# Filler products, halved first loads, a reordered projection tail and an explicit function-table load in the first part of a two-layer decoder kernel

## The chip, the core and the metric

The kernel runs on one core of one Trainium2 chip. The metric is the device time of one execution in microseconds (us), taken as the median of several runs. Engines are named as the profile names them: PE (TensorE, matrix products and transposes), PEld (its weight loads), ACT (ScalarE), DVE (VectorE), POOL (GpSimd) and SP (SyncE, which issues the DMAs).

## What is computed

Two layers over 256 tokens of width 1024, in float32. Layer 0 is attention (three groups of four dilated-window heads and one group of differential heads, all with normed queries and keys) and a dense SwiGLU. Layer 1 is a gated linear recurrence (HGRN2) and a mixture of 8 experts of which each token takes 2. Cut to its frame, the reference is:

```python
for layer in range(DEPTH):
    if layer % 2 == 0:
        h = h + dilated_diff_mixer(rms_norm(h, attn_norm[j]), attn_w_in[j], ..., attn_w_out[j], layer)
        h = h + swiglu(rms_norm(h, ffn_norm[j]), ffn_w_gate[j], ffn_w_up[j], ffn_w_down[j])
    else:
        h = h + hgrn2_mixer(rms_norm(h, hgrn_norm[j]), hgrn_w_in[j], hgrn_lb_logits, ..., layer)
        h = h + moe_swiglu(rms_norm(h, moe_norm[j]), moe_w_router[j], moe_w_gate[j], ...)

# in the mixer of layer 0
dq = rms_norm(dq.reshape(B, S, N_DIL_HEADS, HEAD_DIM), dil_q_gain)   # the same for dk, fq, fk
p = jnp.exp(s - lse[..., None])
diff = rms_norm(diff, diff_out_gain) * (1.0 - lam_init)
return mixed @ w_out
```

## The kernel before

The 256 tokens are two blocks of 128 (`t` = 0, 1). Every large product is made of three: the weights are split into a rounded part `w_hi` (an ACT copy of 128x1024, L91) and the rest `w_lo` (a DVE subtraction, L91), the inputs into `xh` and `xl`, and `mm3` (L101 to L103) multiplies `xh` with `w_hi`, `xh` with `w_lo` and `xl` with `w_hi`. The weights stream in through SP's queue into `raw` buffers.

**Opening.** The parameters (`rows`) and `x` are loaded, each block of `x` is turned by PE (`to_T`, L285) and its eight 128x128 tiles are scaled and split by ACT and DVE (L291, L292). The first projection (group 0 of the attention) has eight steps `k`; the products of `k` 0 to 3 are held back until step 3, and run for block 0 first, then block 1 (`late` in `pair_steps`). The root mean square of each row of `x` (`rms`, Squares on ACT at L275 whose main result is thrown away into a PSUM bank) is computed behind the turning of block 1.

**Attention.** Four groups of heads. While PE runs the projection of group g+1 (512-wide products), the attention of group g is woven in between (`weave`, by a table of costs). A group's `norms` takes for each block t: a Square of the projected queries and keys (`sq`, L458) and a copy (`qk`, L460) on ACT, the sum per head on DVE, then `root` (L255): Ln (L259) and Exp (L260) on ACT and three small DVE operations give the reciprocal root, and a DVE multiplication (L467) scales `qk`. Then `turn` transposes both blocks on PE (L481). Groups 0 to 2 run `norms` inside the weave; group 3 runs it after the projections, together with the merge of groups 0 to 2 (whose transposed result is `xh` at L294), and calls `root` twice more after its value products (L566 onward).

**Function tables.** ACT evaluates Ln, Exp, Silu and Sigmoid from a set of tables that must be resident. A load of such a set is an instruction of its own, ACT_TABLE_LOAD. The program asks for one set by name at its start, `natural_log_exp_and_others`, which has Ln and Exp. All other loads are put in when the program is compiled, ahead of an activation whose function is not in the set that is resident there. Calls through `table_fn` and `table_set` carry an order token, by which they keep their order among themselves; plain `nc.scalar.activation` calls, as in `root` and in the softmax, carry none.

**Stage ends.** Attention, dense layer and HGRN end in the same way: `row_tail` runs the last two steps of the output projection into four PSUM banks `acc[t][c]` (block t, column half c), and `norm_T` adds the result to `h`, takes the Squares of each row (L275, into a bank of the pair `pj`) and turns the rows into the next stage's `xh` and `xl` (L285, L294). The next stage's first products go to `pj` banks.

**Routing.** `route` computes for each token its two experts, its place in each expert's list (`place`) and a table `info`, then the first one-hot matrix (`oneh`, L1087) starts the experts.

What sets the order on an engine is a scheduler that takes the program's order, data dependencies and tokens; an instruction with no dependency may be placed far ahead of where it is written.

Of the kernel before, what the change touches and what calls it, by code (L numbers as in the profile page):

```python
# [8 lines left out]
F32 = mybir.dt.float32  # L9
# [30 lines left out]
def tile_trunk(  # L40
# [59 lines left out]
    def mm3(ps, xh, xl, wh, wl, first, last, chk=False):  # L100
        nc.tensor.matmul(ps, lhsT=xh, rhs=wh, start=first, stop=False, skip_group_check=chk)  # L101
        nc.tensor.matmul(ps, lhsT=xh, rhs=wl, start=False, stop=False, skip_group_check=chk)  # L102
        nc.tensor.matmul(ps, lhsT=xl, rhs=wh, start=False, stop=last, skip_group_check=chk)  # L103
# [5 lines left out]
    def pair_steps(xh, xl, w, c0, c1, ps, late=False, raw=None, ready={}):  # L109
# [4 lines left out]
        def step(k):  # L114
# [6 lines left out]
            if not late or k >= KT // 2:  # L121
                part(k, 0)
                part(k, 1)
            elif k == KT // 2 - 1:
                for t in range(NT):
                    for j in range(KT // 2):
                        part(j, t)

        def part(k, t):
            mm3(ps[t], xh[:, k, TOK[t]], xl[:, k, TOK[t]], *box[k], k == 0, k == KT - 1)  # L130
# [35 lines left out]
    def row_tail(xh, xl, wv, k0, acc, last, kx=0, first=False, between=None):  # L166
# [56 lines left out]

    def load_params(pool):
# [45 lines left out]
    def rms(t):  # L270
# [3 lines left out]
        for c in range(2):  # L274
            nc.scalar.activation(bank("pj"), h[t][:, HALF[c]], AF.Square, accum_out=ss[:, c:c + 1])  # L275
# [27 lines left out]
    def norm_T(hgs, gain, acc, into=None):  # L303
# [3 lines left out]
        for t in range(NT):  # L307
# [3 lines left out]
            r, pw = rms(t)  # L311
# [5 lines left out]
    def along(pool, rs):  # L317

        ps = bank("tp")
        for t in range(NT):  # L320
            diag = pool.tile([P, P], F32, name="diag", tag="diag", bufs=1)
            nc.vector.tensor_scalar(diag, ident, rs[t], None, op0=ALU.mult)
            nc.tensor.matmul(ps[:, TOK[t]], lhsT=ones, rhs=diag, start=t == 0, stop=True, skip_group_check=True)
        row = pool.tile([P, S], F32, name="row", tag="row", bufs=1)
# [36 lines left out]
    with tc.tile_pool(name="att", bufs=2) as att, tc.tile_pool(name="atc", bufs=1) as atc:  # L361
        w_in = attn_w_in[0]
        rows, lam_in = load_params(att)
        turn_params(rows)
        for c in range(2):
            nc.sync.dma_start(out=h[0][:, HALF[c]], in_=x[0, TOK[0], HALF[c]])
        first = pair_load((w_in, w_in), 0, 768, 0)
        nc.sync.dma_start(out=h[1], in_=x[0, TOK[1], :])
        xh, xl = x_tiles()
        last = to_T(h[0], xh, xl, 0, 0, 8, gain=GAIN_A)  # L370
        with behind(last):
            ready = {k: split(first[:, k:k + 2], [2, 2, 256]) for k in (0, 2)}
# [5 lines left out]
        gain_f = gain_tile(ffn_norm, pws[1])  # L378

        r2 = []  # L380
# [999 lines left out]
```

## Time and profile before

| | |
|---|---|
| median of 3 runs | 1488.56 us (1488.22 to 1489.09) |
| the profiled execution | 1489.99 us |
| its span in the trace | 1488.3 us |
| mean granted clock of PE | 0.996 of full speed |
| busy: PE, DVE, ACT, POOL | 1453.3, 1213.9, 1035.2, 31.9 us |
| moved by DMA | 434.05 MB, 292 GB/s on average |

All durations below come from the profiled execution, which is 1.43 us above the median; 1.7 us of it lie outside the span. The attention runs until about 158 us and the dense layer until about 350 us; the recurrence and the experts take the rest. PE is busy 98% of the span, so nearly all that can be won or lost by order lies in the stretches in which PE waits: the opening, the attention, and the passages from one stage to the next. The rows that matter stand two sections below.

### The profile page before, as it was taken

The numbers are of one execution on the slowest core, as the hardware profiler recorded it, in microseconds if no ns is written. First come the engines' busy times: TensorE is split into PE (matmuls) and PEld (weight loads), VectorE is DVE, ScalarE is ACT, GpSimd is POOL, SyncE is SP. The second block draws the span as 40 slices with busy tenths as digits, with TensorE's granted clock in tenths as the row PEclk, the third lists the DMA queues.
The fourth block names the chain that finished last, engine by engine and source line by source line (L and its number), as shares of the span: only waits on it lengthen the run. The fifth ranks groups of instructions, "written<-read, shape, count | busy, mean of one in ns | idle before, by whom it ended". The sixth has DMA issues, their size and how long they took to land.

```text
span 1488.3 us, 20143 instructions
## 1 busy us (share of the span) xinstructions
PE 1453.3 (98%) x7509; PEld 1216.6 (82%) x7509; DVE 1213.9 (82%) x1460; ACT 1035.2 (70%) x1285; POOL 31.9 (2%) x45
## 2 busy tenths in 40 slices
PE   7999999999999999999999999999999999999996
PEld 6887899998889788888888878888877888887885
DVE  7775656557867899999989888889888888888885
ACT  6655544445766688888878777777777777778774
POOL 1000000000000100000000000000000000000000
PEclk9999999999999999999999999999999999999999
DMA  9933355656454499999999999999999999999971
GB/s 315 369 125 114 128 182 187 186 183 183 142 170 142 143 348 365 384 370 385 379 348 376 356 351 395 360 353 360 374 367 373 381 366 350 356 371 362 391 262 16
DMA packets 209691, 434.05 MB, mean 292 GB/s; under 512 B 7402, under 2 KB 58642, under 8 KB 209586
## 3 DMA queue, kind: packets, MB, share of 16 engines
q1 hardware_dynamic: 207506, 425.77, 79.6%
q0 software_dynamic: 2080, 6.92, 2.3%
q8 instruction: 61, 1.00, 0.3%
q14 instruction: 44, 0.36, 0.1%
HBM read 427.41 MB, written 5.24 MB: 291 GB/s over the span
## 4 chain that ended last, share of the span: by engine, by line
issue 53%; PE 37%; DMA 5%; DVE 2%; ACT 2%; POOL 0%; SPq 0%; POOLq 0%; ACTq 0%; DVEq 0%
PE acc L101 5%; PE acc L102 5%; PE acc L103 5%; DMA out_dram<-y,idx 4%; PE pj L342 3%; PE pj L344 3%; PE pj L343 3%; PE pj L101 2%; PE pj L103 2%; PE pj L102 2%; DVE w_lo L91 1%; PE pj L760 1%; PE pj L761 1%; PE pj L762 1%; PE tp L556 1%
## 5 line engine op out<-in xcount | busy, mean ns | idle before, releaser
L91 DVE TENSOR_TENSOR w_lo<-raw,w_hi 128x1024 fp32r<-128x1024 f32 x810 | 956.8, 1221 | 169.2 <-ACT w_hi L91 153.5
L91 ACT ACTIVATE w_hi<-raw 128x1024 fp32r<-128x1024 f32 x810 | 830.0, 1057 | 248.4 <-PE acc L103 82.9
L102 PE MATMUL acc<-w_lo,xgh 128*128 128x512 f32 x904 | 357.9, 396 | 0.0
L101 PE MATMUL acc<-w_hi,xgh 128*128 128x512 f32 x904 | 354.2, 392 | 1.0 <-ACT xgh L294 1.0
L103 PE MATMUL acc<-w_hi,xgl 128*128 128x512 f32 x904 | 353.2, 391 | 0.0
L102 PEld LDWEIGHTS acc<-w_lo,xgh 128*128 128x128 f32 x904 | 169.6, 188 | 51.8 <-DVE w_lo L91 14.6
L101 PEld LDWEIGHTS acc<-w_hi,xgh 128*128 128x128 f32 x904 | 169.8, 188 | 37.1 <-ACT xgh L294 1.2
L103 PEld LDWEIGHTS acc<-w_hi,xgl 128*128 128x128 f32 x904 | 169.8, 188 | 33.0
L102 PE MATMUL pj<-w_lo,hh 128*128 128x512 f32 x448 | 177.8, 397 | 0.0
L103 PE MATMUL pj<-w_hi,hl 128*128 128x512 f32 x448 | 174.9, 390 | 0.0
L101 PE MATMUL pj<-w_hi,hh 128*128 128x512 f32 x448 | 158.1, 391 | 0.7 <-ACT hh L1177 0.5
L101 PEld LDWEIGHTS pj<-w_hi,hh 128*128 128x128 f32 x448 | 84.1, 188 | 19.6 <-ACT hh L1177 0.9
L103 PEld LDWEIGHTS pj<-w_hi,hl 128*128 128x128 f32 x448 | 84.2, 188 | 16.3
L102 PEld LDWEIGHTS pj<-w_lo,hh 128*128 128x128 f32 x448 | 84.2, 188 | 16.3
L342 PE MATMUL pj<-xh,w_hi 128*128 128x256 f32 x320 | 90.8, 284 | 0.6 <-DVE hm L677 0.6
L343 PE MATMUL pj<-xl,w_hi 128*128 128x256 f32 x320 | 90.5, 283 | 0.0
L344 PE MATMUL pj<-xh,w_lo 128*128 128x256 f32 x320 | 90.5, 283 | 0.0
L1163 ACT ACTIVATE sg<-acc 128x512 f32<-128x512 f32 x55 | 32.9, 598 | 52.8 <-PE acc L103 52.8
L1177 ACT ACTIVATE hh<-tp 128x512 fp32r<-128x512 f32 x56 | 33.4, 596 | 49.8 <-PE pj L102 43.4
L342 PEld LDWEIGHTS pj<-xh,w_hi 128*128 128x128 f32 x320 | 61.4, 192 | 1.2 <-DVE hm L677 0.8
L343 PEld LDWEIGHTS pj<-xl,w_hi 128*128 128x128 f32 x320 | 61.4, 192 | 0.4
L344 PEld LDWEIGHTS pj<-xh,w_lo 128*128 128x128 f32 x320 | 61.4, 192 | 0.0
(300 smaller groups left out, 1594.3 us busy)
## 6 DMA issues: line engine op xcount, KB each, us to landing
raw<-in_moe_w_gate_dram SPq DMA_DIRECT2D x112, 1024.0 KB, 7.4
raw<-in_moe_w_up_dram SPq DMA_DIRECT2D x112, 1024.0 KB, 7.9
raw<-in_moe_w_down_dram SPq DMA_DIRECT2D x110, 1024.0 KB, 7.6
raw<-in_ffn_w_gate_dram SPq DMA_DIRECT2D x22, 512.0 KB, 3.8
raw<-in_ffn_w_up_dram SPq DMA_DIRECT2D x22, 512.0 KB, 4.8
raw<-in_ffn_w_down_dram SPq DMA_DIRECT2D x11, 1024.0 KB, 4.8
raw<-in_hgrn_w_in_dram SPq DMA_DIRECT2D x10, 1024.0 KB, 5.5
raw<-in_attn_w_in_dram SPq DMA_DIRECT2D x16, 512.0 KB, 9.3
```

Of the source, the lines that this page charges most:

```text
L91: split.last = nc.scalar.activation(hi, view, AF.Copy), nc.vector.tensor_sub(lo, view, f32(hi))
L101: nc.tensor.matmul(ps, lhsT=xh, rhs=wh, start=first, stop=False, skip_group_check=chk)
L102: nc.tensor.matmul(ps, lhsT=xh, rhs=wl, start=False, stop=False, skip_group_check=chk)
L103: nc.tensor.matmul(ps, lhsT=xl, rhs=wh, start=False, stop=last, skip_group_check=chk)
L342: nc.tensor.matmul(o, lhsT=wh[:, i, j], rhs=xh[:, k], start=k == 0 and j == 0, stop=False, skip_group_check=True)
L343: nc.tensor.matmul(o, lhsT=wh[:, i, j], rhs=xl[:, k], start=False, stop=False, skip_group_check=True)
L344: nc.tensor.matmul(o, lhsT=wl[:, i, j], rhs=xh[:, k], start=False, stop=k == KT - 1, skip_group_check=True)
L556: nc.tensor.matmul(po[:, j * 64:(j + 1) * 64], lhsT=pT[:, kb, j, :], rhs=v[:, kb, j * 64:(j + 1) * 64], start=(j == 0 and kb == 0), stop=( ...
L760: nc.tensor.matmul(o, lhsT=wh[:, k], rhs=xh[:, k], start=first, stop=False, skip_group_check=True)
L761: nc.tensor.matmul(o, lhsT=wh[:, k], rhs=xl[:, k], start=False, stop=False, skip_group_check=True)
L1163: nc.scalar.activation(self.sg, ps, AF.Silu)
L1177: nc.scalar.activation(self.hh, ptv, AF.Copy)
```

## The change

It touches the opening, the stage ends, the routing and the calls that name function tables. Line numbers shift by 4 to 18, so L458 of before is L462 of the changed kernel, L259 and L260 are L268 and L269, and L275 is L284.

- **Opening.** The first weights come in four DMAs (two k halves of two column pieces) and `h[1]` in two. Eleven small products of the identity matrix with itself, whose result nobody reads (`busy`), run on PE: three ahead of the parameters' transposition and eight after block 0 of `x`. The turning of block 1 moves from ahead of the first products to between those of block 0 and those of block 1. The root mean square of the rows and the small parameters move behind the projection of group 0.
- **Stage ends.** `row_tail` finishes column half 0 (both steps) before half 1. The Squares in `norm_T` write to `acc` banks, except at the end of HGRN, where they keep `pj`. `along` uses the two halves of `row` in place of one buffer `diag`.
- **Tables.** Silu and the router's Sigmoid are called through `table_fn`, and the set `silu_and_others` is asked for by name at the start of the dense layer and in `route`.
- **Routing.** `place` is computed for both blocks in five operations, two copies into `info` move into the first expert's step, and so does the largest count.

```diff
+        return nc.tensor.matmul(ps, lhsT=xl, rhs=wh, start=False, stop=last, skip_group_check=chk)
...
             elif k == KT // 2 - 1:
-                for t in range(NT):
-                    for j in range(KT // 2):
-                        part(j, t)
+                for j in range(KT // 2):
+                    done = part(j, 0)
+                if between:
+                    with tc.issue_after(done.ins):
+                        between()
+                for j in range(KT // 2):
+                    part(j, 1)
...
-            for i in range(2):
-                k = k0 - kx + i
-                for c in range(2):
+            for c in range(2):
+                for i in range(2):
+                    k = k0 - kx + i
                     mm3(acc[t][c], xh[:, k, TOK[t]], xl[:, k, TOK[t]], ws[i][0][:, HALF[c]], ws[i][1][:, HALF[c]],
                         first and i == 0, last and i == 1)
...
+    def busy(n):
+        for _ in range(n):
+            nc.tensor.matmul(bank("tp")[:, 0:P], lhsT=ident, rhs=ident, start=True, stop=True)
...
-    def rms(t):
+    def rms(t, junk=("pj", 2)):
...
-    def norm_T(hgs, gain, acc, into=None):
+    def norm_T(hgs, gain, acc, into=None, junk=("acc", 4)):
...
+        row = pool.tile([P, S], F32, name="row", tag="row", bufs=1)
         for t in range(NT):
-            diag = pool.tile([P, P], F32, name="diag", tag="diag", bufs=1)
-            nc.vector.tensor_scalar(diag, ident, rs[t], None, op0=ALU.mult)
-            nc.tensor.matmul(ps[:, TOK[t]], lhsT=ones, rhs=diag, start=t == 0, stop=True, skip_group_check=True)
...
+        busy(3)
         turn_params(rows)
...
-        first = pair_load((w_in, w_in), 0, 768, 0)
-        nc.sync.dma_start(out=h[1], in_=x[0, TOK[1], :])
+        wv = w_in.rearrange("(kt p) c -> p kt c", p=P)
+        first = load([4, 2, 256], lambda r: [(r[:, k:k + 2, i, :], wv[:, k:k + 2, c:c + 256])
+                                             for k in (0, 2) for i, c in enumerate((0, 768))])
+        for c in range(2):
+            nc.sync.dma_start(out=h[1][:, HALF[c]], in_=x[0, TOK[1], HALF[c]])
         xh, xl = x_tiles()
         last = to_T(h[0], xh, xl, 0, 0, 8, gain=GAIN_A)
+        busy(8)
...
-        with behind(split.last):
-            last = to_T(h[1], xh, xl, 1, 0, 8, gain=GAIN_A)
-        with behind(last):
-            rx, pws = zip(*[rms(t) for t in range(NT)])
-            small_params(lam_in)
...
         weave(groups[0].project(), [])
+        with behind(turned[0]):
+            rx, pws = zip(*[rms(t) for t in range(NT)])
+            small_params(lam_in)
...
     with tc.tile_pool(name="ffn", bufs=2) as ffn:
+        table_set("silu_and_others")
...
-                nc.scalar.activation(g, g, AF.Silu)
+                table_fn(g, g, AF.Silu)
...
-            nc.scalar.activation(g2[:, 0:1], dv, AF.Sigmoid)
-            nc.scalar.activation(g2[:, 1:2], dv, AF.Sigmoid, scale=-1.0)
+            table_fn(g2[:, 0:1], dv, AF.Sigmoid)
+            table_fn(g2[:, 1:2], dv, AF.Sigmoid, scale=-1.0)
...
+        table_set("silu_and_others")
```

Three places show how the change moves instructions. **ACT, from the program's first instruction to the end of the splitting of block 1 of `x`** (`xh` are the turned tiles of `x`, `w_hi` the rounded weights). Before:

```order
L198 ACT_TABLE_LOAD
L291 ACTIVATE xh<-tp,cols 128x128 x8
L91 ACTIVATE w_hi<-raw 128x1024 x2
L291 ACTIVATE xh<-tp,cols 128x128 x2
L91 ACTIVATE w_hi<-raw 128x1024 x2
L291 ACTIVATE xh<-tp,cols 128x128 x4
L91 ACTIVATE w_hi<-raw 128x1024
L291 ACTIVATE xh<-tp,cols 128x128 x2
```

Now:

```order
L202 ACT_TABLE_LOAD x2
L300 ACTIVATE xh<-tp,cols 128x128 x8
L91 ACTIVATE w_hi<-raw 128x1024 x4
L300 ACTIVATE xh<-tp,cols 128x128 x6
L91 ACTIVATE w_hi<-raw 128x1024
L300 ACTIVATE xh<-tp,cols 128x128 x2
```

The row of table loads at the head has one load more: the set asked for at the start of the dense layer stands right behind the set asked for at the program's start. Four weight copies now stand ahead of the tiles of block 1, where two stood.

**ACT, the norms of group 1** (`sq` and `qk` from the projected queries and keys, then Ln and Exp of `root` for block 0 and block 1). Before:

```order
L458 ACTIVATE sq<-acc 128x512
L460 ACTIVATE qk<-acc 128x512
L458 ACTIVATE sq<-acc 128x512
L259 ACTIVATE root<-qss 128x8
L460 ACTIVATE qk<-acc 128x512
L260 ACTIVATE root<-root 128x8
L91 ACTIVATE w_hi<-raw 128x1024
L259 ACTIVATE root<-qss 128x8
L260 ACTIVATE root<-root 128x8
L91 ACTIVATE w_hi<-raw 128x1024 x2
L483 ACTIVATE qT<-tp,cols 128x2x128 x2
```

Now:

```order
L462 ACTIVATE sq<-acc 128x512
L268 ACT_TABLE_LOAD
L268 ACTIVATE root<-qss 128x8
L464 ACTIVATE qk<-acc 128x512
L269 ACT_TABLE_LOAD
L269 ACTIVATE root<-root 128x8
L91 ACTIVATE w_hi<-raw 128x1024
L268 ACT_TABLE_LOAD
L268 ACTIVATE root<-qss 128x8
L269 ACT_TABLE_LOAD
L269 ACTIVATE root<-root 128x8
L91 ACTIVATE w_hi<-raw 128x1024 x2
```

Each Ln (L268) and each Exp (L269) has a table load of its own ahead of it: four in the norms of a group, two in each of the two roots behind the value products of group 3, 20 in all. One more load stands ahead of the Exp of the small parameters, one more at the program's head, and the one that stood at the attention's end now stands at the dense layer's end. The whole listing has 38 loads, against 17 before.

**ACT, from the dense layer's last splits to HGRN's inputs** (Squares of the rows into a discarded bank, then the turned `xh`). Before:

```order
L91 ACTIVATE w_hi<-raw 128x1024 x2
L275 ACTIVATE pj,ss<-h_77 128x512 x2
L91 ACTIVATE w_hi<-raw 128x1024 x2
L294 ACTIVATE xh<-tp 128x4x128 x2
L275 ACTIVATE pj,ss<-h_78 128x512 x2
L294 ACTIVATE xh<-tp 128x4x128 x2
```

Now:

```order
L91 ACTIVATE w_hi<-raw 128x1024 x2
L284 ACTIVATE acc,ss<-h_77 128x512 x2
L91 ACTIVATE w_hi<-raw 128x1024
L303 ACTIVATE xh<-tp 128x4x128 x2
L284 ACTIVATE acc,ss<-h_78 128x512 x2
L91 ACTIVATE w_hi<-raw 128x1024
L303 ACTIVATE xh<-tp 128x4x128 x2
```

One weight copy fewer stands ahead of the first pair of `xh`, one now stands behind the second Squares, and the Squares write to `acc` in place of `pj`.

## Rows read from the trace of the kernel before

**Rows 1.** The profile's page, part 1: engine, busy time, share of the span, instructions

```profile
PE 1453.3 (98%) x7509; PEld 1216.6 (82%) x7509; DVE 1213.9 (82%) x1460; ACT 1035.2 (70%) x1285; POOL 31.9 (2%) x45
```

**Rows 2.** Waits of PE: engine, line, releaser, total us, times, longest

```profile
PE pj L101 <- ACT pj L275: 3.3, 2, 1.9
...
PE acc L1122 <- DVE oneh L1087: 1.3, 1, 1.3
```

**Rows 3.** Stretches at the attention's end: length, busy us (count) per engine, then PE's granted clock

```profile
142.00:144.00 2.00, 1.31 (x8) 0.94 (x8) 1.54 (x3) 1.96 (x3) 0.00 (x0) 1.00 0.00 0
144.00:152.00 8.00, 7.39 (x28) 6.14 (x29) 2.18 (x9) 1.25 (x4) 0.00 (x0) 0.57 0.41 131
```

**Rows 4.** Groups of instructions of ACT: table loads of the whole run

```profile
L195 ACT ACT_TABLE_LOAD x14 | 18.0, 1283 | 5.5 <-DVE ce L834 5.3
```

**Rows 5.** Timeline of ACT, second stage: start us, us, engine, line

```profile
377.70 1.28 ACT L195 ACT_TABLE_LOAD   x1
378.99 1.09 ACT L195 ACTIVATE s<-s,lb,om 128x256 f32<-128x256 f32 x2
```

**Rows 6.** Timeline of ACT, the norms of group 1

```profile
55.57 0.20 ACT L259 ACTIVATE root<-qss 128x8 f32<-128x8 f32 x1
...
57.20 0.20 ACT L259 ACTIVATE root<-qss 128x8 f32<-128x8 f32 x1
57.43 0.21 ACT L260 ACTIVATE root<-root 128x8 f32<-128x8 f32 x1
```

**Rows 7.** Timeline of DVE, the same norms, second token block

```profile
58.80 0.16 DVE L261 SCALAR_TENSOR_TENSOR root<-root 128x8 f32<-128x8 f32 x1
...
59.82 1.22 DVE L91 TENSOR_TENSOR w_lo<-raw,w_hi 128x1024 fp32r<-128x1024 f32 x1
60.95 0.75 DVE L467 SCALAR_TENSOR_TENSOR qk<-qk,rs,qss 128x512 f32<-128x512 f32 x1
```

**Rows 8.** Timeline of PE, the transposes that wait for them

```profile
62.01 1.04 PE L481 MATMUL tp<-ident,qk 128*128 128x128 f32 x8
```

**Rows 9.** Timeline of all engines, the norms of group 0

```profile
31.85 0.60 ACT L458 ACTIVATE sq<-acc 128x512 f32<-128x512 f32 x1 [0.80 <-DVE tab L412]
...
36.81 0.21 ACT L260 ACTIVATE root<-root 128x8 f32<-128x8 f32 x1
...
37.45 0.66 PE L481 MATMUL tp<-ident,qk 128*128 128x128 f32 x4 [0.28 <-DVE qk L467]
...
39.31 0.75 DVE L467 SCALAR_TENSOR_TENSOR qk<-qk,rs,qss 128x512 f32<-128x512 f32 x1
```

**Rows 10.** Timeline of ACT, the norms of group 3

```profile
110.39 0.21 ACT L260 ACTIVATE root<-root 128x16 f32<-128x16 f32 x1
111.89 0.87 ACT L294 ACTIVATE xh<-tp 128x512 fp32r<-128x512 f32 x2 [1.29 <-PE tp L285]
```

**Rows 11.** Timeline of ACT, the roots after the values of group 3

```profile
134.71 0.20 ACT L259 ACTIVATE root<-dss 128x4 f32<-128x4 f32 x1 [1.56 <-DVE dss L566]
```

**Rows 12.** Timeline of ACT, the opening

```profile
10.91 2.00 ACT L91 ACTIVATE w_hi<-raw 128x1024 fp32r<-128x1024 f32 x2 [1.49 <-DMA raw<-in_attn_w_in_dram]
...
15.22 2.00 ACT L91 ACTIVATE w_hi<-raw 128x1024 fp32r<-128x1024 f32 x2 [0.60 <-DMA raw<-in_attn_w_in_dram]
```

**Rows 13.** Timeline of all engines, the opening's first products

```profile
13.87 1.20 PE L101 MATMUL acc<-w_hi,xh 128*128 128x512 f32 x2
...
18.24 0.39 PE L101 MATMUL acc<-w_hi,xh 128*128 128x512 f32 x1
...
26.92 0.28 PE L101 MATMUL acc<-w_hi,xh 128*128 128x256 f32 x1
```

**Rows 14.** Timeline of PE, start of the dense layer

```profile
158.11 0.50 PE L101 MATMUL pj<-w_hi,xh 128*128 128x512 f32 x1 [1.41 <-ACT pj L275]
```

**Rows 15.** Timeline of all engines, end of the dense layer

```profile
347.83 1.03 PE L285 MATMUL tp<-ident,wide 128*128 128x128 f32 x8
...
350.78 0.51 PE L101 MATMUL pj<-w_hi,xh 128*128 128x512 f32 x1 [1.92 <-ACT pj L275]
```

More of the change, by code (lines that the diff above doesn't have):

```diff
@@ L107, in pair_load, with pair_steps @@
         return load([4, 2, 256], lambda r: [(r[:, :, i, :], wv[i][:, k:k + 4, c:c + 256]) for i, c in enumerate((c0, c1))])
-    def pair_steps(xh, xl, w, c0, c1, ps, late=False, raw=None, ready={}):
+    def pair_steps(xh, xl, w, c0, c1, ps, late=False, raw=None, ready={}, between=None):
         box = {}
@@ L274, in rms @@
         for c in range(2):
-            nc.scalar.activation(bank("pj"), h[t][:, HALF[c]], AF.Square, accum_out=ss[:, c:c + 1])
+            nc.scalar.activation(bank(*junk), h[t][:, HALF[c]], AF.Square, accum_out=ss[:, c:c + 1])
         nc.vector.tensor_scalar(rs, ss[:, 0:1], ss[:, 1:2], 1.0 / D, op0=ALU.add, op1=ALU.mult)
@@ L319, in along @@
         ps = bank("tp")
+        row = pool.tile([P, S], F32, name="row", tag="row", bufs=1)
         for t in range(NT):
-            diag = pool.tile([P, P], F32, name="diag", tag="diag", bufs=1)
-            nc.vector.tensor_scalar(diag, ident, rs[t], None, op0=ALU.mult)
-            nc.tensor.matmul(ps[:, TOK[t]], lhsT=ones, rhs=diag, start=t == 0, stop=True, skip_group_check=True)
-        row = pool.tile([P, S], F32, name="row", tag="row", bufs=1)
+            nc.vector.tensor_scalar(row[:, TOK[t]], ident, rs[t], None, op0=ALU.mult)
+        for t in range(NT):
+            nc.tensor.matmul(ps[:, TOK[t]], lhsT=ones, rhs=row[:, TOK[t]], start=t == 0, stop=True, skip_group_check=True)
         nc.scalar.activation(row, ps[:, 0:S], AF.Copy)
@@ L440, in qk @@
                         box["s"] = pair_steps(xh, xl, (w_in, w_in), self.cs[0], self.cs[1], self.pqk, late=self.g == 0,
-                                              **(dict(raw=first, ready=ready) if self.g == 0 else {}))
+                                              **(dict(raw=first, ready=ready, between=turn_second) if self.g == 0 else {}))
                     box["s"][k][1]()
@@ L604, in tile_trunk @@
         weave(groups[0].project(), [])
+        with behind(turned[0]):
+            rx, pws = zip(*[rms(t) for t in range(NT)])
+            small_params(lam_in)
+        gain_f = gain_tile(ffn_norm, pws[1])
+        r2 = []
+        for t in range(NT):
+            r = atc.tile([P, 2], F32, name=f"r2{t}")
+            nc.vector.tensor_mul(r[:, 0:1], rx[t], rx[t])
+            nc.vector.tensor_scalar(r[:, 1:2], r[:, 0:1], 1.0 / 32, None, op0=ALU.mult)
+            nc.vector.tensor_scalar(r[:, 0:1], r[:, 0:1], 1.0 / 64, None, op0=ALU.mult)
+            r2.append(r)
         tables()
@@ L674, in act @@
                     g = ffn.tile([P, 256], F32, name="g", tag="g")
-                    nc.scalar.activation(g, self.pg[t][:, 0:256], AF.Silu, scale=rx[t])
+                    table_fn(g, self.pg[t][:, 0:256], AF.Silu, scale=rx[t])
                     hm = ffn.tile([P, 256], F32, name="hm", tag="u")
@@ L984, in tile_trunk @@
     dense = slot_tiles(S)
-    _, _, rx, pw = norm_T(hg_, gain_m, acc, into=dense)
+    _, _, rx, pw = norm_T(hg_, gain_m, acc, into=dense, junk=("pj", 2))
     for t in range(NT):
@@ L1256, in up @@
             super().up()
+            with tc.issue_after(split.last[1].ins):
+                nc.vector.tensor_reduce(out=cmax, in_=count, axis=AX.X, op=ALU.max)
+                nc.vector.tensor_copy(cmax_i, cmax)
     def run_jobs(jobs):
```

46 lines of the change are left out of this document (19 added, 27 removed).

## The prediction

> **What bounds the kernel now.** I read the page first: PE is busy 1453.3 us of the span, 98% [rows 1], so the kernel is bound by PE, and what an order can change is the time in which PE stands. The list of PE's waits says for whom. The two waits for the discarded Squares of the rows, 3.3 us in all, and the one for the first one-hot matrix, 1.3 us [rows 2], are those that the edits to the stage ends and to the routing touch. Then I looked at PE's clock by stretches. It is at full speed nearly everywhere, but at the attention's end it falls: in 142 to 144 us PE is busy 1.31 of 2.00 us, and in the 8 us that follow the granted clock is 0.57 [rows 3]. Of TensorE's two levels, 2.4 and 1.2 GHz, that is the lower one for about 8 x 0.43 / 0.5 = 6.9 us, and work that takes 6.9 us there would take 3.4 us at the higher one. So a fall like that one costs up to 3.4 us, and it came after PE had stood between short products.
>
> The edits that look large (halved loads, fillers, the tail by column halves) work on small waits. The one that looks like a formality does not: the order of the changed kernel shows the set asked for at the dense layer's start at the very head of the program, because nothing ties it to the attention. The set with Ln and Exp is gone before it is used, and every root in the attention now pays two loads. The sum rests on that.
>
> **The loads.** Before, 14 loads stand at the calls by `table_fn`, mean 1283 ns [rows 4]. Seen from the engine, the one at 377.70 us delays the next activation to 378.99 us [rows 5]: 1.29 us a load. In the same place the Trainium skill ("ScalarE: Activation LUTs", section "What ACT_TABLE_LOAD costs") gives 1283 ns for the load and about 1380 ns more for a drain, 2.66 us in all; the row agrees with the first figure and shows nothing of the second. By that figure the stalls below would about double.
>
> Group 1, from its rows: the chain runs from the first Ln at 55.57 us over the second Ln to the second Exp, which starts at 57.43 us [rows 6]. Four loads stand in it now, 4 x 1.29 = 5.2 us, so that Exp starts at 62.6 us and ends at 62.8. Behind it DVE takes from its first small operation at 58.80 us to the next weight split at 59.82 us, 1.0 us, then that split, then the scaling, which ends at 60.95 + 0.75 = 61.70 us [rows 7]: 2.9 us from the first operation. DVE is idle for a part of the wait, so I count this once more in full: the scaled block 1 is there at about 65.9 us. PE's eight transposes begin at 62.01 us and take 1.04 [rows 8]; the four of block 0 don't wait, so PE stands from about 62.5 us. That is a stall of about 3.4 us, and since a load also ends the overlap of one activation with the next, I take 3.5. Its bounds are 0 (if the weave finds products to put ahead) and 5.2, all loads in full. The norms of group 2 have the same listing in the same weave: 3.5 as well, with the same bounds.
>
> Group 0 has a later start to gain back: its first Square, at 31.85 us, waited for the ALiBi tables on DVE; its second Exp started at 36.81 us, PE's first four transposes ran at 37.45 us, and block 1 was scaled at 39.31 + 0.75 = 40.06 us [rows 9]. In the changed order the tables stand further ahead, so the chain can start when the last 512-wide product of the projection has drained, at about 27.9 us. It then takes 36.81 - 31.85 = 5.0 us as before, five loads (6.4 us, one of them for the small parameters), so the second Exp starts at about 39.2 us, and 3.2 us later, as before, block 1 is scaled: 42.4 us. PE asks for it at about 38.0: 4.4 us of stall (0 to 6.4).
>
> Group 3: four loads put the end of its second Exp from 110.60 to 115.8 us, and behind it stand the copies of the merged heads, which started at 111.89 us [rows 10] and which PE's next products need. 115.8 - 111.9 = 3.9 us (0 to 5.2). The two roots behind the value products are hidden: ACT stood 1.56 us before the first Ln, at 134.71 us [rows 11], which covers the first load, since a load waits for no data; for the second I count nothing, as PE has other products there. If that cover is gone it costs 1.29 each. The load at the program's head lies ahead of the first data, and costs nothing.
>
> Sum of the loads: 4.4 + 3.5 + 3.5 + 3.9 = 15.3 us.
>
> **The clock.** Each of these stalls is longer than the idle time in rows 3 after which the clock fell, and each is followed by products that would run at the lower level. No row shows a stall of 4 us in the middle of 512-wide products, so the cost lies between 0 and 4 x 3.4 = 13.6 us. I take two falls of half that size, 2 x 1.7 = 3.4 us, nearer to nothing because the work on either side of these stalls is dense, where that of rows 3 was thin.
>
> **The opening.** ACT splits the first two weight parts from 10.91 us, and the second two from 15.22 us, when their DMA landed [rows 12]. Before, PE turned block 1 first and began its products at 13.87 us; between there and 18.24 us 11 products took 0.40 us each, and the other 37 of the 48 up to 26.92 us took 0.235 each [rows 13]. Now the first product can start at about 10.91 + 1.0 = 11.9 us. Twelve at 0.43 bring it to 17.1; then eight transposes, 1 us; but ACT has all four splits ahead of the tiles of block 1, until 15.22 + 2.00 = 17.2 us. Block 1 is split from about 18.2, its products begin at about 18.9, and 36 of 0.235 end at 27.3 us: 0.4 later than before (-1.0 if the clock rises earlier through the fillers and the earlier start, +1.5 if the tiles come one by one). The eleven fillers run while PE waits for data; if that cover were gone, 11 at the price of a transpose would be about 1.4 us.
>
> **The stage ends.** At the dense layer's start PE waited 1.41 us for the Square that held its `pj` bank [rows 14]. With the Squares in `acc` banks, the next thing it needs is the split of the inputs, about half of that later than the bank it asked for; I count -0.7 (0 to -1.4). At the dense layer's end the wait was 1.92 us, at 350.78 us, behind transposes that began at 347.83 [rows 15], and one weight copy fewer stands ahead of the first inputs: -1.3 (0 to -1.9). For the column-half order of the tail I count nothing beyond this: it frees the first half's sum earlier for the additions on DVE, which the inputs then wait for in turn. At the routing DVE has about six small operations fewer ahead of the one-hot matrix, but a copy stands between its two halves now: -0.3 of the 1.3 (0 to -1.0). `along` has its next waiting reader elsewhere: nothing. Behind the routing nothing changes. Sum -2.3 us.
>
> **Total.** 15.3 + 3.4 + 0.4 - 2.3 = +16.8 us. Against the profiled execution, 1489.99 us (span 1488.3 and 1.7 around it), that gives 1506.8; the median lies 1.43 us lower, and on it the forecast is 1488.56 + 16.8 = 1505.4 us.
>
> **Rivals.** (1) No fall of the clock: 13.4 us of loss, about 1502 us. For it speaks that the products around the stalls are dense; against it rows 3. (2) A fall after each stall, at 3.4 us each: 13.4 + 13.6 would be 1515.6 us; with falls of half to full size I place it at 1512. (3) A load costs twice the 1.29 us of the row, if the engine must also run empty around it. That puts 4 x 1.29 = 5.2 us more on each of the four chains, up to 21 us: about 1525. Against it stands that the activation behind the load started with no such gap [rows 5]. (4) The other side: the loads are in the listing, but cost PE nothing, because the weave moves enough products ahead of the transposes or because one load serves Ln and Exp together. Then the edits' gains remain; at their full bounds, -1.0, -1.4, -1.9 and -1.0, these are 5.3 us: 1483.3 us, faster. It decides at the point where the four stalls together fall below 5.3 - 3.0 = 2.3 us, some 0.6 us each; group 1 alone has a slack of 62.5 - 61.7 = 0.8 us against 5.2 us of loads. The Trainium skill (the same page, section "Table sets: the hidden batching unit") states that Ln and then Exp need one load, since one set has both; by that rule ten loads would go, and group 1's chain would be 2.6 us later, not 5.2. The changed order speaks against it: a load stands ahead of each of the two. (5) The loads are hidden and the gains are those of the sum, 0.4 - 2.3 = -1.9 us: 1486.7 us, which can't be told from no change; a few us of stall on top would end there too.
>
> **How the numbers follow.** The forecast with one to three falls of the clock: 0.57. No fall: 0.15. A fall each time: 0.10. Loads at twice the price: 0.06. Hidden with full gains: 0.06. Hidden, about the same: 0.06. A measurement of this kernel can tell about 0.2% (3 us) from no change, so "same" is 1485.6 to 1491.5 us. Faster 0.06, same 0.06, slower 0.88. The range takes in the forecast, the two clock cases and stalls a third shorter (15.3 x 2/3 gives 1500): 1496 to 1514.
>
> **What would show it.** Right: some 20 table loads on ACT between 25 and 150 us in the changed trace, in pairs around Ln and Exp; PE waits at the transposes of the scaled `qk` of groups 0 to 2 of 3 to 5 us each, and one at the merged heads of group 3; a granted clock below 1.00 in some stretches behind them. The waits for the discarded Squares gone or halved. Wrong: loads without waits of PE (the weave covers them), or a load of more than 1.3 us to the next activation, or PE's time at 160 us less than 12 us behind that of before.

## The result

The changed kernel takes 1510.3 us (median of 4 runs, 1508.67 to 1510.72) against 1488.5 us: slower by 21.8 us, a ratio of 1.0144 (95% interval 1.0126 to 1.0161). The forecast was 1505.4 us with a range of 1496 to 1514. The sign, the mechanism and the range hold; the sum was 5 us short, and the runs below find where for the larger part.

The page of the changed kernel, part 1 (engine, busy time, share, instructions), answers to [rows 1]:

```profile
span 1508.3 us, 20210 instructions
PE 1464.2 (97%) x7531; PEld 1223.3 (81%) x7531; DVE 1213.0 (80%) x1456; ACT 1060.8 (70%) x1306; POOL 31.5 (2%) x45
```

The span is 20 us longer. PE's busy time grew by 10.9 us, of which the 22 passes of the eleven fillers are 5.9 us. ACT's busy time grew by 25.6 us. The groups of table loads on ACT (line, count, busy us, mean ns, idle time before) say where from, and answer to [rows 4]:

```profile
L199 ACT ACT_TABLE_LOAD x14 | 18.0, 1283 | 6.5 <-DVE ce L851 5.3 <-PE pj L103 1.0
L268 ACT ACT_TABLE_LOAD x10 | 12.8, 1283 | 0.2
L269 ACT ACT_TABLE_LOAD x10 | 12.8, 1283 | 0.2
L202 ACT ACT_TABLE_LOAD x3 | 3.8, 1283 | 0.8 <-PEq L1385 0.8
L256 ACT ACT_TABLE_LOAD x1 | 1.3, 1283 | 0.0
```

Ten loads at the Ln of `root` and ten at its Exp, one at the small parameters, three at the sets asked for by name, and 14, as before, at the calls by `table_fn`: 38, as the order had it. The waits of PE (engine, line, releaser, us in total, times, longest) answer to [rows 2]:

```profile
PE tp L485 <- DVE qk L471: 10.9, 3, 3.8
...
PE tp L294 <- DVE mixed L602: 2.6, 1, 2.6
PE tp L294 <- DVE mixed L572: 1.6, 1, 1.6
...
PE pj L351 <- DVE hm L694: 1.3, 1, 1.3
...
PE acc L1140 <- DVE oneh L1105: 0.7, 1, 0.7
...
PE pj L101 <- ACT xh L303: 0.7, 2, 0.4
```

The first line is the loss: three waits at the transposes of the scaled `qk`, 10.9 us, where the kernel before had one of 0.3. The next two are group 3, and are not among the waits of before: the merged heads, and a root behind the value products. The waits for the discarded Squares (3.3 us before) are gone; 0.7 us for the next thing, the split inputs, took their place. The wait for the one-hot matrix fell from 1.3 to 0.7. Two others grew: for the dense layer's first hidden values (`hm`) from 0.6 to 1.3, and for `sg` near HGRN's start from 0.2 to 1.1.

Group 1 shows the chain as [rows 6] showed it. ACT in the changed kernel (start us, us, engine, line):

```profile
59.33 0.60 ACT L462 ACTIVATE sq<-acc 128x512 f32<-128x512 f32 x1 [1.07 <-PE tp L560]
...
62.07 1.28 ACT L268 ACT_TABLE_LOAD   x1
63.37 0.21 ACT L268 ACTIVATE root<-qss 128x8 f32<-128x8 f32 x1
...
64.08 1.28 ACT L269 ACT_TABLE_LOAD   x1
65.37 0.21 ACT L269 ACTIVATE root<-root 128x8 f32<-128x8 f32 x1
...
66.55 1.28 ACT L268 ACT_TABLE_LOAD   x1
67.84 0.21 ACT L268 ACTIVATE root<-qss 128x8 f32<-128x8 f32 x1
68.07 1.28 ACT L269 ACT_TABLE_LOAD   x1
69.37 0.21 ACT L269 ACTIVATE root<-root 128x8 f32<-128x8 f32 x1
```

The same Square in the kernel before:

```profile
52.95 0.60 ACT L458 ACTIVATE sq<-acc 128x512 f32<-128x512 f32 x1 [1.07 <-PE tp L556]
```

From the Square of block 0 to the second Exp it is 59.33 to 69.37 us, 10.0 us; before, 52.95 to 57.43, 4.5 us. Four loads added 5.6 us, 1.39 each: the load's 1.28 and the overlap of neighbours that it ends. On PE, behind it (with [idle time before <- releaser]):

```profile
72.66 1.09 PE L485 MATMUL tp<-ident,qk 128*128 128x128 f32 x4 [3.56 <-DVE qk L471]
...
73.97 0.63 PE L102 MATMUL acc<-w_lo,xh 128*128 128x512 f32 x1
```

A stall of 3.56 us, and then 512-wide products of 0.63 us where they took 0.39. That is the clock, and the busy time by stretches (length, busy us and count of PE, PEld, DVE, ACT, POOL, then PE's granted clock, DMA share, GB/s) shows it four times:

```profile
40.00:50.00 10.00, 6.84 (x33) 4.71 (x33) 8.75 (x18) 4.14 (x7) 0.00 (x0) 0.83 1.06 382
70.00:80.00 10.00, 7.34 (x30) 5.42 (x32) 7.03 (x15) 3.36 (x5) 0.00 (x0) 0.66 0.34 114
100.00:110.00 10.00, 6.89 (x25) 5.29 (x26) 6.97 (x16) 3.82 (x6) 0.00 (x0) 0.66 0.33 107
130.00:140.00 10.00, 6.93 (x31) 5.33 (x31) 6.02 (x15) 7.38 (x12) 0.00 (x0) 0.83 0.24 78
```

In the kernel before, the clock in the stretch with the transposes of group 1 is 1.00:

```profile
60.00:70.00 10.00, 9.86 (x57) 7.28 (x56) 8.58 (x19) 5.17 (x15) 0.00 (x0) 1.00 1.08 361
```

Behind each of the four stalls the granted clock is below 1.00. At the lower of the two levels, half speed, (1 - clock) x 10 / 0.5 gives 3.4, 6.8, 6.8 and 3.4 us, 20.4 us in all; products in it lose up to half of that, 10.2 us. The prediction counted 3.4. A fifth fall (0.83 from 20 to 30 us) lies in the opening of this execution, ahead of all the stalls.

### The profile page after: what moved, and what is told of

Read it like the earlier page. It is cut to its first block, busy times and chain, and to the rows that moved or that the text cites. A ratio compares the mean times of both kernels' runs of the same rounds, so it can differ in the third digit from the quotient of the medians.

```text
span 1508.3 us, 20210 instructions
## 1 busy us (share of the span) xinstructions
PE 1464.2 (97%) x7531; PEld 1223.3 (81%) x7531; DVE 1213.0 (80%) x1456; ACT 1060.8 (70%) x1306; POOL 31.5 (2%) x45
## 4 chain that ended last, share of the span: by engine, by line
issue 52%; PE 17%; DMA 4%; DVE 1%; ACT 1%; POOL 0%; POOLq 0%; DVEq 0%; ACTq 0%
DMA out_dram<-y,idx 4%; PE acc L101 2%; PE acc L102 2%; PE acc L103 2%; PE pj L101 2%; PE pj L103 2%; PE pj L102 2%; PE pj L777 1%; PE pj L778 1%; PE pj L779 1%; PE tp L894 0%; PE acc L1140 0%; PE tp L923 0%; PE tp L881 0%; PE tp L917 0%
## 5 line engine op out<-in xcount | busy, mean ns | idle before, releaser
L101 PE MATMUL acc<-w_hi,xh 128*128 128x512 f32 (+1 forms) x160 | 61.5, 385 | 2.8 <-ACT xh L303 1.2
```

## The experiments

**One line taken out.** `e1_no_set` is the changed kernel without the asking for the Silu set at the dense layer's start.

```diff
     with tc.tile_pool(name="ffn", bufs=2) as ffn:
-        table_set("silu_and_others")
```

> The changed kernel without the one line that asks for the Silu set at the dense layer's start; everything else stays. Theory (that line alone costs the time, through the table loads in the attention): the 20 loads at the roots are gone, the waits for the scaled qk fall from 10.9 us to under 1 us, and the time is 1486 to 1489 us (the opening 1.9 us later than before, the stage ends some 2 us shorter). Rival (the opening, the column-half tail or the other banks carry a large part of the loss): 1495 us or more, with waits of PE left that before did not have.

Measured: 1485.41 us, ratio to before 0.9975 (0.9965 to 0.9986), just under the range of the theory. The rival falls. One line costs 24.9 us, and all the other edits together gain 3.1. In the trace PE does not wait for `qk` at all, the table loads are 16, and the passages between stages look like this (PE, first products of the dense layer and of HGRN):

```profile
154.84 0.50 PE L101 MATMUL pj<-w_hi,xh 128*128 128x512 f32 x1 [0.28 <-ACT xh L303]
...
346.40 0.50 PE L101 MATMUL pj<-w_hi,xh 128*128 128x512 f32 x1 [0.39 <-ACT xh L303]
```

**The line alone.** `e2_set_only` is the kernel before with that line and with Silu through `table_fn`.

```diff
+        table_set("silu_and_others")
...
-                nc.scalar.activation(g, g, AF.Silu)
+                table_fn(g, g, AF.Silu)
...
-                    nc.scalar.activation(g, self.pg[t][:, 0:256], AF.Silu, scale=rx[t])
+                    table_fn(g, self.pg[t][:, 0:256], AF.Silu, scale=rx[t])
```

> The kernel before with the asking for the Silu set at the dense layer's start alone, and Silu called in token order. Theory: all of the loss and none of the small gains, 1508 to 1513 us, with three waits of about 3.6 us at the transposes of qk and a lower granted clock behind each. Rival (the loads only hurt together with the changed opening and order): under 1500 us.

Measured: 1510.65 us, ratio 1.0141 (1.0124 to 1.0159), with the same waits on PE (line, releaser, us in total, times, longest); those for `mixed`, 2.6 and 1.6 us, are there too:

```profile
PE tp L481 <- DVE qk L467: 10.3, 4, 3.6
```

So the line carries the loss in either surrounding: +22.1 us here, +24.9 in the changed kernel. That the line does it is settled from both sides; that it does it by where its load stands is the next run's question.

**The line where it was written.** `e3_set_tied` keeps the line and ties it behind the last Exp of a root.

```diff
-        nc.scalar.activation(r, r, AF.Exp, scale=-0.5)
+        root.last = nc.scalar.activation(r, r, AF.Exp, scale=-0.5)
...
-        table_set("silu_and_others")
+        with tc.issue_after(root.last.ins):
+            table_set("silu_and_others")
```

> The changed kernel with the asking for the Silu set tied behind the last Exp of a root in the attention, so that the load cannot go to the program's head. Theory (only where the load stands does the harm): as without the line, 1485 to 1489 us, and the first hidden values of the dense layer come up to 1.3 us earlier, since their load is done ahead of time. Rival (a load at the end of the attention delays the Squares and inputs that stand behind it on ACT): 1 to 1.3 us slower than without the line.

Measured: 1485.23 us, ratio 0.9969 (0.9958 to 0.998). The load as such does no harm; its place did. (The trace has 16 table loads, none of them at a root.) The wait for the dense layer's first hidden values (1.28 us at 168.95 us without the line) is not among the waits of this trace. In the median the gain over the kernel without the line, 0.2 us, can't be told from nothing.

**The clock in the stalls.** To part the stall from the clock, PE is kept busy while it waits: products of the identity that nobody reads, between the transposes of block 0 and of block 1.

```diff
+NFILL = (24, 24, 24)
...
-                        nc.tensor.transpose(out=pt[:, i * P:(i + 1) * P], in_=self.qk[t][:, i * P:(i + 1) * P], identity=ident)
+                        tr = nc.tensor.transpose(out=pt[:, i * P:(i + 1) * P], in_=self.qk[t][:, i * P:(i + 1) * P], identity=ident)
...
+                    if t == 0 and self.g < 3:
+                        with tc.issue_after(tr.ins):
+                            ps = bank("pj")
+                            for _ in range(NFILL[self.g]):
+                                tr = nc.tensor.matmul(ps[:, 0:P], lhsT=ident, rhs=ident, start=True, stop=True)
```

> The changed kernel with 24 products of the identity with itself, read by nobody, put between the transposes of block 0 and of block 1 in groups 0 to 2, where PE stands 3.6 to 3.8 us. The stalls stay, but PE works in them. Theory (of the about 6.2 us that each group costs, some 2.5 are TensorE's clock, which falls because PE stood): the granted clock stays at 1.00 behind groups 0 to 2, and the time falls by 6 to 7.5 us, to 1503 to 1504.5. Rival (the rest beyond the stall is ACT and DVE running late with weight splits, not the clock): within 1 us of 1510 us, or slower.

Measured: 1509.46 us (1507.9 to 1510.33), 0.8 less than the changed kernel, which its spread (1508.67 to 1510.72) doesn't tell from nothing. As it stands this looks like the rival's result, but the fillers were too long: each runs as two passes, and 24 of them took 5.5 us, 1.9 us more than the stall. The clock stayed at 1.00 from 30 to 120 us, so it seems that what the clock gave back the fillers took. Hence 15 of them:

```diff
-NFILL = (24, 24, 24)
+NFILL = (15, 15, 15)
```

> As the kernel with 24 fillers, with 15: in that trace each filler was two passes of 0.115 us, so that 24 took 5.5 us where PE stands 3.6 to 3.8; 15 take 3.45 us and fit. The granted clock stayed at 1.00 behind groups 0 to 2 there. Theory (clock): the loss of a group falls from about 6.2 us to the stall, 3.6 to 3.8 us; three groups give 7 us, so 1503 to 1504 us. Rival (the rest is late weight splits): 1508 to 1510 us.

Measured: 1505.2 us (1504.86 to 1505.8), ratio 1.0107 (1.0092 to 1.0122): 5.1 us less. PE in group 1, and the stretches behind groups 0 to 2:

```profile
66.62 3.51 PE L494 MATMUL pj<-ident 128*128 128x128 f32 x30
70.34 0.63 PE L486 MATMUL tp<-ident,qk 128*128 128x128 f32 x4 [0.20 <-DVE qk L472]
```

```profile
40.00:50.00 10.00, 8.76 (x53) 6.25 (x52) 9.29 (x19) 4.56 (x15) 0.00 (x0) 1.00 1.06 380
70.00:80.00 10.00, 9.66 (x58) 7.03 (x57) 8.25 (x21) 5.72 (x17) 0.00 (x0) 1.00 0.67 216
100.00:110.00 10.00, 9.92 (x60) 7.72 (x59) 7.56 (x22) 4.47 (x13) 0.00 (x0) 1.00 0.56 182
```

The fillers fit (0.20 us of wait is left), and the clock stays at full speed. The best measure of a group is the time from its first Square to that of the next group. The first Squares of groups 1 and 2 in `e1_no_set`, of group 2 in the changed kernel (group 1 is at 59.33, above), and of both here:

```profile
51.98 0.60 ACT L462 ACTIVATE sq<-acc 128x512 f32<-128x512 f32 x1 [1.07 <-PE tp L560]
76.42 0.60 ACT L462 ACTIVATE sq<-acc 128x512 f32<-128x512 f32 x1 [1.07 <-PE tp L560]
```

```profile
89.78 0.60 ACT L462 ACTIVATE sq<-acc 128x512 f32<-128x512 f32 x1 [1.07 <-PE tp L560]
```

```profile
57.02 0.60 ACT L463 ACTIVATE sq<-acc 128x512 f32<-128x512 f32 x1 [1.07 <-PE tp L566]
85.21 0.60 ACT L463 ACTIVATE sq<-acc 128x512 f32<-128x512 f32 x1 [1.08 <-PE tp L566]
```

From group 1 to 2 it is 24.44 us in `e1_no_set`, 30.45 in the changed kernel and 28.19 here; from group 2 to 3 it is 29.03, 35.33 and 32.79. So a group loses 6.0 to 6.3 us, of which 3.75 remain with the clock held, the stall and its fringe, and 2.3 to 2.5 us are the clock. The forecast of 7 us for three groups was missed by 2: group 0 gave less, from 30.13 to 29.58 by the same measure. The three together are 5.35 us, near the 5.1 of the medians. Group 3 has no fillers here, so the price of its fall is not measured.

**One group alone.** `e11_one_group` is the kernel before, with the set of Ln and Exp given up for group 1 only.

```diff
+        last_exp = [None]
...
+                if self.g in (1, 2):
+                    with tc.issue_after(last_exp[0].ins):
+                        table_set("silu_and_others" if self.g == 1 else LOG_EXP)
...
-                        nc.scalar.activation(sc[:, o, b, :], src[o][:, b, :], AF.Exp, bias=nm[:, o, b:b + 1],
+                        last_exp[0] = nc.scalar.activation(sc[:, o, b, :], src[o][:, b, :], AF.Exp, bias=nm[:, o, b:b + 1],
```

> The kernel before with the set of Ln and Exp given up in group 1 alone: the Silu set is asked for behind the last softmax Exp of group 0 and the set of Ln and Exp behind that of group 1, so that the four roots' activations of group 1 have a load each and no other group has. Theory (each group pays for itself: about 3.7 us of stall and 2.3 to 2.5 us of clock): 6.0 us more than before, 1494 to 1495 us, with one wait of 3.5 us and one stretch of lower clock. Rival (the falls of the clock come from the repeated stalls together): only the stall, 1492 us.

Measured: 1494.21 us, ratio 1.0041 (1.0025 to 1.0057), 5.9 us more than before. One stall (PE), and one fall of the clock behind it:

```profile
65.02 0.63 PE L486 MATMUL tp<-ident,qk 128*128 128x128 f32 x4 [3.98 <-DVE qk L472]
```

```profile
56.00:64.00 8.00, 5.04 (x26) 3.94 (x24) 4.01 (x12) 7.68 (x12) 0.00 (x0) 1.00 1.09 349
64.00:72.00 8.00, 6.98 (x34) 4.91 (x35) 5.90 (x14) 2.51 (x7) 0.00 (x0) 0.79 1.07 366
```

Each group pays for itself; the fall doesn't need a row of stalls. From the first Square of group 1 to that of group 2 this trace takes 29.42 us, against 24.32 in the kernel before, 5.1 us more; the medians give 5.9.

**The opening.** Three variants of the kernel without the line: the opening of before, no fillers, and block 1 turned ahead of the products.

```diff
 # e4_old_opening
...
-        first = load([4, 2, 256], ...)
...
+        first = pair_load((w_in, w_in), 0, 768, 0)
...
 # e6_no_fillers
-        busy(3)
...
-        busy(8)
...
 # e5_turn_first
...
-        def turn_second():
-            turned.append(to_T(h[1], xh, xl, 1, 0, 8, gain=GAIN_A))
+        with behind(split.last):
+            turned = [to_T(h[1], xh, xl, 1, 0, 8, gain=GAIN_A)]
...
```

> The changed kernel without the asking for the Silu set, and with the opening of before (one load of each pair, block 1 turned ahead of the products, no fillers, the mean squares behind the turning). Theory (the new opening is worth nothing on average: the first 256-wide product of the attention's first value projection began at 26.8 to 28.9 us in four traces with it and at 26.6 and 26.9 us in two without): 1485 to 1486 us, as with it. Rival: the fillers and halves are worth 1 to 2 us, 1486.5 to 1487.5 us.

> The changed kernel without the asking for the Silu set, and without the eleven fillers of the opening. Theory (the fillers raise the clock ahead of the first products, whose durations then are 0.77, 0.55 and 0.39 us where before they were 0.63 for eleven products; but the products of block 1 wait for its tiles, so the gain is spent there): 1485 to 1486.5 us, first products at 0.63 us. Rival (the fillers carry the opening): 1487 us or more.

> The changed kernel without the asking for the Silu set, and with block 1 of x turned ahead of the first products, fillers and halved loads kept. Theory (the moved turning opens a hole of 0.8 to 1.7 us in front of block 1's products, and here it is gone): the value projection of group 0 starts 0.5 to 1 us earlier, 1484.5 to 1485 us. Rival (the first products then wait for block 1's load, as before): no gain or 1 us later, 1485.5 to 1486.5 us.

Measured: 1485.88 us (ratio 0.9979, 0.9968 to 0.999), 1487.19 us (0.9985, 0.9975 to 0.9995) and 1485.28 us (0.9978, 0.9969 to 0.9988), against 0.9975 with the new opening. The opening of before can't be told from the new one. Without the fillers the median is 1.8 us later, which is the rival's number. But the interval overlaps that with them and that of the opening of before, so a worth of the fillers is not shown. Block 1 turned first comes out between its two expectations. On PE the fillers give with one hand and take with the other. Without them, the first product begins early, and the products of block 0 run at the lower clock:

```profile
10.50 0.79 PE L101 MATMUL acc<-w_hi,xh 128*128 128x512 f32 x1 [3.83 <-ACT w_hi L91]
...
12.41 0.63 PE L103 MATMUL acc<-w_hi,xl 128*128 128x512 f32 x1
```

In the changed kernel, with them, the third product already takes 0.39 us. But the eight fillers hold PE for 4.21 us, and the first product begins 2.1 us later than without them. Then the products of block 1 wait for its tiles, and in this execution the clock falls again right there:

```profile
8.76 4.21 PE L231 MATMUL tp<-ident 128*128 128x128 f32 x16 [2.74 <-DVE xl L301]
12.62 0.77 PE L101 MATMUL acc<-w_hi,xh 128*128 128x512 f32 x1
...
13.58 0.39 PE L103 MATMUL acc<-w_hi,xl 128*128 128x512 f32 x1
...
17.82 0.50 PE L101 MATMUL acc<-w_hi,xh 128*128 128x512 f32 x1 [0.90 <-ACT xh L300]
...
19.62 0.50 PE L103 MATMUL acc<-w_hi,xl 128*128 128x512 f32 x1 [0.83 <-DVE xl L301]
...
28.86 0.28 PE L101 MATMUL acc<-w_hi,xh 128*128 128x256 f32 x1
```

The clock rises at another point in each execution: in the trace of `e1_no_set`, with the same fillers, five products still take about 0.63 us. Block 0's last product begins at 16.25 us without fillers, at 15.66 in the changed kernel and at 17.05 in `e1_no_set`, so what they win or lose there differs from one execution to the next.

With block 1 turned first those waits are gone and the value projection starts at 25.87 us in its trace, earlier than in the eight traces with the whole new opening (26.09 to 28.86, 27.35 on average), but not than in the four with the opening of before (25.40 to 26.92, 26.38 on average). In the time of the whole kernel that microsecond can't be seen.

**The stage ends.** `e7_old_tail` undoes the column-half order, `e8_squares_pj` puts the Squares back into `pj`; both without the line.

```diff
 # e7_old_tail
-            for c in range(2):
-                for i in range(2):
-                    k = k0 - kx + i
+            for i in range(2):
+                k = k0 - kx + i
+                for c in range(2):
...
 # e8_squares_pj
-    def norm_T(hgs, gain, acc, into=None, junk=("acc", 4)):
+    def norm_T(hgs, gain, acc, into=None, junk=("pj", 2)):
```

> The changed kernel without the asking for the Silu set, and with row_tail in its old order (step by step, both halves in each). Theory (of the stage ends' gain the banks carry all, as the prediction counted): 1485 to 1486 us, the waits at the next stage's first products at 0.3 to 0.4 us. Rival (the inputs come earlier only because the first half's sum is done earlier): 1486.5 to 1488 us, with those waits at 1 us or more.

> The changed kernel without the asking for the Silu set, and with the Squares back in the pj banks. Theory (banks): the waits for the Squares come back, 1.1 us at the dense layer's start and 1.3 at its end, and the time is 1487.5 to 1488 us. Rival (the column-half order has moved the sums so far ahead that the banks are free in time): 1485 to 1486 us.

Measured: 1487.67 us (0.9988, 0.9978 to 0.9997) and 1488.32 us (0.9993, 0.9984 to 1.0002). PE's first products of the dense layer and of HGRN, with the old tail:

```profile
153.28 0.50 PE L101 MATMUL pj<-w_hi,xh 128*128 128x512 f32 x1 [0.94 <-ACT xh L303]
...
344.94 0.50 PE L101 MATMUL pj<-w_hi,xh 128*128 128x512 f32 x1 [0.82 <-ACT xh L303]
```

and with the Squares in `pj`:

```profile
156.76 0.50 PE L101 MATMUL pj<-w_hi,xh 128*128 128x512 f32 x1 [1.41 <-ACT pj L284]
...
349.11 0.50 PE L101 MATMUL pj<-w_hi,xh 128*128 128x512 f32 x1 [1.43 <-ACT pj L284]
```

With both edits the waits are 0.28 and 0.39 us. The banks take away the wait for the Squares (1.1 and 1.0 us at the two places), as expected. The tail order was expected to be worth nothing and is worth 0.7 and 0.4 us of wait at these two: once the banks are free, the inputs are next, and they come earlier when the first column half is summed earlier. So for the tail it is the rival that holds, in its cause and its time; the waits, 0.94 and 0.82 us, stay a little under the 1 us that it named. In the medians the two cost 2.3 and 2.9 us, more than these waits; both intervals overlap that of `e1_no_set`, so the waits are shown, and their full price is not. From HGRN's first product to the end of the span, the traces of before and of `e1_no_set` take the same 1137.5 us: what the routing's shorter wait gained is not there in the sum, and the longer wait for `sg` (0.9 us more) is of the size to take it.

**The clock at the attention's end.** The fall of [rows 3] is there in some executions and not in others: the trace of `e8_squares_pj` has it (0.60 from 142 to 150 us), that of `e7_old_tail` has 1.00 there. `e12_fill_end` is `e3_set_tied` with six fillers in PE's waits there.

```diff
+NEND = (4, 2)
...
+    def fill(n, ps):
+        for _ in range(n):
+            nc.tensor.matmul(ps[:, 0:P], lhsT=ident, rhs=ident, start=True, stop=True)
...
+                        if g == 3 and t == 1 and kb == 0 and j == 2:
+                            with tc.issue_after(self.tr.ins):
+                                fill(NEND[0], bank("tp"))
...
+                if g == 3 and t == 1:
+                    with tc.issue_after(self.tr.ins):
+                        fill(NEND[1], po)
```

> The kernel with the Silu set tied behind the last Exp, and six fillers at the attention's end, where PE waits 0.9 and 0.6 us between the transposes and the values of group 3 (four and two, at 0.23 us each). In the traces so far the granted clock fell there in some executions and not in others, and runs of one kernel lie up to 4 us apart. Theory (the fall there comes from PE standing in those waits): no fall in the trace, the runs within 1.5 us of each other, the median 1483 to 1484 us. Rival (the fall comes from the thin work around the waits, which fillers this small don't change): as without, about 1485 us with the same spread.

Measured: 1484.03 us, runs from 1483.27 to 1485.96, ratio 0.9966 (0.9953 to 0.9979). The stretch in question, with the clock at 1.00 before the last two numbers:

```profile
142.00:150.00 8.00, 6.16 (x44) 5.21 (x44) 3.38 (x9) 4.45 (x10) 0.00 (x0) 1.00 0.40 131
```

This fits the theory, but `e3_set_tied` had no fall in its trace either, and the spread (2.7 us in five runs against 4.0 in ten) narrowed less than expected; in this trace a fall in the opening remains (0.79 from 16 to 24 us). That the fillers hold the clock there is not shown. By the median it is the fastest kernel of the study, 4.3 us under before, but not to be told from `e3_set_tied`.

## Why the prediction came out as it did

- **The hoisted set and the loads: right.** The loads stand where the order put them. The load's price, 1.29 us, was a little low: on the chain of group 1 each costs 1.39 us. No drain on the scale of the 1380 ns that the Trainium skill ("ScalarE: Activation LUTs", section "What ACT_TABLE_LOAD costs") adds to a load is seen; by an estimate from its 2.66 us a load, the four would have put the second Exp 10.6 us later, and it is 5.6. The Trainium skill (the same page, section "Table sets: the hidden batching unit") states that Ln and then Exp need one load, since one set has both. This trace doesn't agree: with the Silu set asked for last, each of the two has a load of its own (ten and ten). The kernel before, which had asked for the joint set and for no other ahead of the attention, has none at its roots.
- **The stalls: right.** Forecast 4.4, 3.5, 3.5 and 3.9 us. Measured 3.80, 3.56 and 3.56 us at the transposes of groups 0 to 2, and for group 3 the 2.6 us at the merged heads with 0.4 us behind it. One part of a step failed: the second root behind the value products was called hidden, and PE waited 1.6 us for its result. By its own rule, 1.29 us if that cover is gone, it was low by 0.3 as well. The sum is 15.6 us against 15.3. At the dense layer's first product PE is 21.3 us behind the kernel before (179.40 against 158.11 us), where less than 12 would have spoken against the prediction.
- **The clock: the mis-sized term.** I took two falls of half size, 3.4 us, "nearer to nothing because the work on either side of these stalls is dense". There was a fall behind each of the four, 20.4 us at the lower level, up to 10.2 us of loss; `e10_fill_shorter` measures 2.3 to 2.5 us for each of groups 1 and 2. The reason given for the small number failed: dense work on both sides did not prevent the fall, neither here nor behind the single stall of `e11_one_group`, and work put into the stall did. The line costs 24.9 us, of which 15.6 are the stalls; 9.3 are left, 5.9 us above the 3.4 counted. With 0.3 more for the stalls and 1.2 more gained by the other edits (3.1 against 1.9) that makes 5.0, the miss. Of the 9.3, `e10_fill_shorter` shows 5.1 to be the clock. The other 4.2 are not parted: the fall behind group 3 was not filled, each stall has a fringe (0.2 us in groups 1 and 2), and in the two traces 2.1 us of the difference lie in the opening, ahead of the first stall, where executions without the line differ by as much.
- **The opening: small, as forecast, its cause only in part.** Forecast +0.4 us with bounds of -1.0 and +1.5. In the profiled execution it was +1.9, outside the bounds: PE stood before block 1's products, and the clock fell there. Over the traces the average is +1.0 (27.35 against 26.38), with ranges that overlap; without the line, exchanging the openings moves the median by 0.5 us the other way (1485.41 and 1485.88). So the sign is open. The fillers were called hidden and priced at 1.4 us; they take 5.9, the eight of them delay the first product, and they raise the clock for the products behind it.
- **The stage ends: right in size, one step wrong.** Forecast -0.7, -1.3 and -0.3. The waits went from 1.41 to 0.28, from 1.92 to 0.39 with 0.20 behind it, and from 1.30 to 0.70: -1.1, -1.3 and -0.6. The tail's column order, counted at nothing, carries a part of it. The two waits that grew, by 0.7 and 0.9 us, were not foreseen. The first is gone where the load for Silu is tied (`e3_set_tied`), but why the two grew is open.
- **The rivals.** Hidden loads are excluded by the two kernels with and without the line, loads at double the price by the 1.39 us each in group 1. A fall of the clock after every stall, put at 0.10 and 1512 us, is what happened, in groups 1 and 2 at about two thirds of the full price of 3.4 us, in group 0 at 0.55 us.

## What to carry to other kernels

A request that has no data dependency, such as a table set asked for by name, belongs behind the last user of what it displaces, by an explicit tie; otherwise the scheduler may put it at the program's head, as here, and everything between pays. Read the order of the changed program for instructions that appear where nobody wrote them: here 20 loads of 1.28 us, one ahead of each Ln and each Exp of a root, cost 25 us, of which only 15.6 were PE's waits. When PE is stalled for 3.6 to 4.0 us amid dense work, as here, count a fall of its clock behind each stall, or give it fillers that are no longer than the wait.

## What the runs showed of the hardware

Each stall of 3.56 to 3.98 us amid 512-wide products (groups 0 to 2 of the changed kernel, group 1 of `e11_one_group`) was followed by a lower granted clock. In groups 1 and 2 the fall added 2.3 and 2.5 us to the 3.75 that a group loses with the clock held. Fillers of 128x128 in float32 run as two passes of about 0.115 us at full speed. Put into the stalls they held the clock at 1.00, but they only paid where they fitted the wait (24: 0.8 us, within the spread; 15: 5.1 us). Executions of one kernel with the same instructions differ by up to 6.3 us (1486.89 to 1493.16 in 18 runs of the kernel before), and the traces of its relatives differ by whether the clock falls at the attention's end.
